# Ordinary units last in each phase, and more weight buffers, in a two-layer decoder trunk on one NeuronCore

## The chip, the cores and the metric

The kernel runs on one core of a Trainium2 chip. The metric is the device time of one execution in microseconds (us). The profile's engine names are PE (TensorE matmul), PEld (its weight loads), DVE (VectorE), ACT (ScalarE), POOL (GpSimd) and SP (SyncE, which issues most DMA here). PEclk is the TensorE clock that was granted, 1.00 being full speed.

## The reference

272 tokens (16 meta tokens and 256 input tokens) of width 2048 pass through two layers, each a token mixer (layer 0: RWKV-7, layer 1: gated linear attention) and a squared-ReLU MLP of hidden width 8192, all in float32:

```
def sq_relu_mlp(x, w1, w2):
    h = jax.nn.relu(x @ w1)
    return (h * h) @ w2

for i in range(DEPTH):                       # DEPTH = 2
    hn = rms_norm(h, norm_mix[i])
    h = h + (rwkv7_time_mix(hn, ...) if i % 2 == 0 else gla_time_mix(hn, ...))
    h = h + sq_relu_mlp(rms_norm(h, norm_mlp[i]), mlp_w1[i], mlp_w2[i])
return rms_norm(h, norm_f)[:, 16:]           # meta tokens dropped
```

Each MLP has two weight matrices of 2048 x 8192 (64 MiB each), so 256 MiB of MLP weights are read in one execution. The change touches the two MLPs and the final norm.

## The kernel before

**Stages.** The first mixer runs to about 592 us, the first MLP (`mlp`, L261) from 592 to 1350, the second mixer to about 1745, the second MLP (`mlp1`, L355) to about 2436, and the final norm and the store end it at 2450.8.

**Split weights.** Products are done to nearly float32 precision with rounded operands. A weight tile `raw` of 128 x 1024 floats (512 KB) is loaded by SP; ScalarE casts it to `hi` (the rounded value); VectorE makes `lo = raw - hi`. The data x is split in the same way, and TensorE adds up hi·xh, hi·xl and lo·xh (`mm3`, L162). So each tile passes DMA, ScalarE, VectorE and TensorE in this order. `wload` (L130) does the first three steps and takes the tiles from pool `wp`: three `raw` buffers and two sets of `hi` and `lo` in the first MLP.

**First MLP.** `up` and `down` go through 64 + 64 rows of output features; a row takes two weight tiles, each with 24 matmuls of 128 x 272: 256 tiles, 6144 matmuls. The order of the instructions on each engine is set by a scheduler that follows data dependences, buffers and priorities. Beside it runs `differences` (L314): for 48 units of the second MLP's w2 it has POOL's queue fetch three operands of 256 KB, VectorE subtract and add them (L335 to L337), and POOL's queue store the three results (`diff`) in memory. `tick` (L297) paces its 51 steps over 118 of the 128 rows; a unit's subtraction is written two steps after its fetch.

**Second MLP.** Here the order is written out. `stream` is a list of slots, each with a weight tile to load and a function that issues its matmuls; the loop at L569 does, for slot i, the functions due before it, the cast and the lo of slot i + 3, the functions due behind it, and the matmuls. There are two kinds of work. A *row* (`row`, L385) makes 128 hidden features: two slots, 16 pairs of matmuls 128 x 512 and 128 x 256 in PSUM bank `own[0]` (or 4), after which VectorE joins the halves (`cj`), squares are made (`F`), and operands for the second product are formed: `HS` with seven combinations for a fast unit, `HC` with four plain blocks for an ordinary one, each with a rounded and a low half. A *unit* (`unit`, L450) multiplies the hidden features of two rows by their part of w2. A *fast* unit does seven products of blocks (Strassen's scheme) instead of eight, with the operands that `differences` stored: banks 1, 2 (`pu`), 6, 7 (`pt`), 5 (`pm`), 3 (`pry`), 4 (`pj`), each product three matmuls. An *ordinary* unit does eight products in two slots, in banks 2, 3, 4 and 0. `FAST` lists the fast ones: 0, 1, 2, 4, 5, 6 of each eight; 3 and 7 are ordinary.

The work is in eight phases, b = 0 to 3 and g = 0, 1 (output columns 0 to 1023 and 1024 to 2047). In a phase, units 0 to 7 add up in their banks. With g = 0, row 10 + p of block b follows unit p for p < 6; with g = 1, row p of block b + 1 stands before unit p, and rows 8 and 9 behind unit 7; the last phase (b = 3, g = 1) has no rows. When the last fast unit is done, ScalarE copies bank 1 (`t1`) and VectorE combines banks 5, 6 and 7 into the result `htok` by eight adds of 128 x 512; after unit 7, it adds banks 2, 3 and 4 to `htok`. Bank 0, which the rows use too, is emptied after each ordinary unit.

**End.** In the last phase each emptied bank is squared and summed for the final norm (`final`, L443); then come, for token half 1 and then 0, sum and rsqrt (L584 to L589), scaling by VectorE and ScalarE (L594, L597) and eight stores (L599). The multiplication of columns 0 to 1023 by the norm's gain `nf` is done early, in `final`, as four operations of 128 x 512.

Of the kernel before, what the change touches and what calls it, by code (L numbers as in the profile page):

```python
# [18 lines left out]
P = 128  # L19
D = 2048  # L20
# [30 lines left out]
FAST = [0, 1, 2, 4, 5, 6]  # L51
# [5 lines left out]
class Kern:  # L57
    def __init__(self, ctx, tc, ap):
# [11 lines left out]
        self.wps = [self.wp]  # L70
# [59 lines left out]
    def wload(self, src, prio=2000):  # L130
        nc = self.nc
        with self.tc.high_priority(offset=prio) if prio else ExitStack():
            raw = self.t(self.wp, [P, 1024], "raw", self.raw_bufs)
# [3 lines left out]
            hi = self.t(pool, [P, 1024], "hi", self.hi_bufs, F32R)  # L137
            lo = self.t(pool, [P, 1024], "lo", self.hi_bufs, F32R)
# [122 lines left out]
    def mlp(self, layer, x, rstd, hres, off, done):  # L261
# [3 lines left out]
        with ExitStack() as es:  # L265
# [27 lines left out]

            steps = self.differences()
# [13 lines left out]
            down(NHB - 1, hid)  # L308

# [45 lines left out]
    def mlp1(self, x, rstd):  # L355
# [14 lines left out]
        hid, parts, before, behind = {}, {}, {}, {}  # L370
# [72 lines left out]
        def final(t, q, late=False):  # L443
# [3 lines left out]
            if not late:  # L447
                tt(h, h, nf[:, 512 * q : 512 * q + 512], ALU.mult)

        def unit(b, g, p):  # L450
# [36 lines left out]

            def pe(k):
                def run(w, slot):
                    H = hid[p]  # L490
                    order = ((2, 3, 4, 0), (2, 3, 0, 4) if end else (0, 2, 3, 4))[k]
                    for at in order:
                        h, ws = {2: (1, one), 0: (0, two), 3: (1, two), 4: (0, one)}[at]
                        product(at, (H[:, 0, 2 * k + h], H[:, 1, 2 * k + h]), w, ws, at == 0 and k == 0,
                                k == 1 and (at == 0 or last))
                    if k == 0:
                        return
                    outs = {2: (1, 0), 3: (1, 1), 0: (0, 1), 4: (0, 0)}
                    for n, at in enumerate(order):
                        if at == 0 or last:  # L500
                            def empty(at=at):
                                add(C[outs[at]], own[at], C[outs[at]])
                                if last and b == NHB - 1 and end:
                                    final(outs[at][0], 2 * g + outs[at][1], True)
# [1211 lines left out]
```

## Time and profile before

| what | us |
|---|---|
| median of 3 runs (lowest, highest) | 2450.61 (2448.34, 2451.45) |
| the profiled execution | 2452.58 |
| its span, first to last instruction | 2450.8 |
| first MLP, 592 to 1350 | 758 |
| one 173 us block of the second MLP: TensorE busy | 163.8 of 173.0 |
| last matmul starts | 2436.47 |

The mean granted TensorE clock is 0.99. A row of groups reads: line, engine, operation, output<-input, shapes, count | busy us, mean ns of one | idle time of the engine just before them <- what ended it. A row of waits: engine, what it was to do, <- what it waited for: us in all, times, longest. Names of tiles are given without their numbers. One line can be that of a helper: all adds of the second MLP carry L357, all casts of it L552.

### The profile page before, as it was taken

The numbers are of one execution on the slowest core, as the hardware profiler recorded it, in microseconds if no ns is written. First come the engines' busy times: TensorE is split into PE (matmuls) and PEld (weight loads), VectorE is DVE, ScalarE is ACT, GpSimd is POOL, SyncE is SP. The second block draws the span as 40 slices with busy tenths as digits, with TensorE's granted clock in tenths as the row PEclk, the third lists the DMA queues.
The fourth block names the chain that finished last, engine by engine and source line by source line (L and its number), as shares of the span: only waits on it lengthen the run. The fifth ranks groups of instructions, "written<-read, shape, count | busy, mean of one in ns | idle before, by whom it ended". The sixth has DMA issues, their size and how long they took to land.

```text
span 2450.8 us, 48648 instructions
## 1 busy us (share of the span) xinstructions
PE 2356.0 (96%) x19205; PEld 2196.8 (90%) x19205; DVE 1829.5 (75%) x3025; ACT 1332.0 (54%) x2075; POOL 206.5 (8%) x469
## 2 busy tenths in 40 slices
PE   9999999999999999999999999999999999998996
PEld 8888898889999999999999999999888888887885
DVE  8778977858666666666666777767678888888888
ACT  6487554666444344344334555655565565565565
POOL 0000000000223322323220000000000000000000
PEclk9999999999999999999999999999999999999998
DMA  6468754535888888888886655556576766676675
GB/s 207 153 214 297 229 168 137 150 103 183 267 291 286 303 286 294 286 296 297 283 280 199 196 175 179 164 166 202 201 233 226 243 226 228 219 250 223 223 249 181
DMA packets 194181, 550.95 MB, mean 225 GB/s; under 512 B 40160, under 2 KB 55776, under 8 KB 193824
## 3 DMA queue, kind: packets, MB, share of 16 engines
q1 hardware_dynamic: 170912, 472.33, 58.3%
q0 software_dynamic: 23040, 75.52, 9.6%
q8 instruction: 150, 2.46, 0.4%
q14 instruction: 79, 0.65, 0.1%
HBM read 493.89 MB, written 52.17 MB: 223 GB/s over the span
## 4 chain that ended last, share of the span: by engine, by line
PE 59%; DVE 18%; DMA 12%; ACT 5%; issue 4%; POOL 2%; SPq 0%; ACTq 0%; DVEq 0%; POOLq 0%
DMA raw<-mlp_w_d 11%; PE pj L396 9%; PE pj L167 9%; PE pj L165 9%; PE pj L166 9%; DVE lo L143 5%; PE pj L397 4%; ACT hi L142 3%; PE pj L198 2%; DVE lo L357 2%; DVE htok L357 1%; POOL x L329 1%; PE pj L199 1%; PE pu L457 1%; PE pu L458 1%
## 5 line engine op out<-in xcount | busy, mean ns | idle before, releaser
L142 ACT CAST hi<-raw 128x1024 fp32r<-128x1024 f32 (+1 forms) x562 | 526.1, 947 | 644.3 <-PE pj L166 364.3
L143 DVE TENSOR_TENSOR lo<-raw,hi 128x1024 fp32r<-128x1024 f32 (+1 forms) x562 | 613.5, 1101 | 336.5 <-ACT hi L142 330.4
L167 PE MATMUL pj<-x,lo 128*128 128x272 f32 (+1 forms) x2560 | 719.5, 281 | 16.3 <-DVE lo L143 15.5
L165 PE MATMUL pj<-x,hi 128*128 128x272 f32 (+1 forms) x2560 | 728.7, 285 | 3.2 <-ACT hi L142 1.6
L166 PE MATMUL pj<-x,hi 128*128 128x272 f32 (+1 forms) x2560 | 713.8, 279 | 0.5 <-DVE x L242 0.5
L167 PEld LDWEIGHTS pj<-x,lo 128*128 128x128 f32 x2560 | 484.8, 189 | 25.8 <-DVE lo L143 24.8
L165 PEld LDWEIGHTS pj<-x,hi 128*128 128x128 f32 x2560 | 484.8, 189 | 16.6 <-issue 6.5
L166 PEld LDWEIGHTS pj<-x,hi 128*128 128x128 f32 x2560 | 485.0, 189 | 3.2 <-issue 1.4
L357 DVE TENSOR_TENSOR lo<-raw,hi 128x1024 fp32r<-128x1024 f32 x352 | 396.5, 1148 | 80.5 <-ACT hi L552 78.5
L552 ACT CAST hi<-raw 128x1024 fp32r<-128x1024 f32 x352 | 338.6, 986 | 142.9 <-PE pj L396 77.8
L396 PE MATMUL pj<-x,hi 128*128 128x512 f32 x1024 | 347.6, 389 | 22.6 <-DVE htok L357 21.4
L167 PE MATMUL pj<-h,lo 128*128 128x272 f32 x1024 | 289.5, 283 | 10.8 <-DVE lo L143 10.0
L165 PE MATMUL pj<-h,hi 128*128 128x272 f32 x1024 | 286.3, 280 | 1.1 <-ACT hi L142 0.9
L166 PE MATMUL pj<-h,hi 128*128 128x272 f32 x1024 | 285.7, 279 | 0.0
L397 PE MATMUL pj<-x,lo 128*128 128x256 f32 x1024 | 282.2, 276 | 0.8 <-DVE lo L357 0.8
L396 PEld LDWEIGHTS pj<-x,hi 128*128 128x128 f32 x1024 | 196.8, 192 | 55.0 <-issue 16.3
L167 PEld LDWEIGHTS pj<-h,lo 128*128 128x128 f32 x1024 | 193.4, 189 | 17.5 <-DVE lo L143 17.2
L397 PEld LDWEIGHTS pj<-x,lo 128*128 128x128 f32 x1024 | 199.7, 195 | 2.2 <-DVE lo L357 1.1
L165 PEld LDWEIGHTS pj<-h,hi 128*128 128x128 f32 x1024 | 193.5, 189 | 2.3 <-ACT hi L142 2.3
L166 PEld LDWEIGHTS pj<-h,hi 128*128 128x128 f32 x1024 | 193.5, 189 | 0.0
L343 POOL DMA_DIRECT2D diff<-x x144 | 78.2, 543 | 129.5 <-DVE x L335 55.9
L198 PE MATMUL pj<-x,hi 128*128 128x512 f32 x256 | 84.1, 382 | 0.1
(361 smaller groups left out, 3450.8 us busy)
## 6 DMA issues: line engine op xcount, KB each, us to landing
raw<-mlp_w_d SPq DMA_DIRECT2D x384, 512.0 KB, 4.9
raw<-gla_in_d SPq DMA_DIRECT2D x98, 512.0 KB, 3.8
raw<-w_rkv_d SPq DMA_DIRECT2D x80, 512.0 KB, 4.4
raw<-w_d SPq DMA_DIRECT2D x80, 512.0 KB, 4.9
x<-w_d POOLq DMA_DIRECT2D x144, 256.0 KB, 5.8
diff<-x POOLq DMA_DIRECT2D x144, 256.0 KB, 6.3
raw<-diff SPq DMA_DIRECT2D x48, 512.0 KB, 5.5
raw<-gla_o_d SPq DMA_DIRECT2D x32, 512.0 KB, 4.3
```

Of the source, the lines that this page charges most:

```text
L142: nc.scalar.copy(hi[:, h], raw[:, h])
L143: nc.vector.tensor_tensor(out=lo[:, h], in0=raw[:, h], in1=hi[:, h].bitcast(F32), op=ALU.subtract)
L165: nc.tensor.matmul(out, hi[:, ws], xh, start=first, stop=False)
L166: nc.tensor.matmul(out, hi[:, ws], xl, start=False, stop=False)
L167: nc.tensor.matmul(out, lo[:, ws], xh, start=False, stop=last)
L198: nc.tensor.matmul(wide, hi[:, ws], xt, start=kt == 0, stop=False)
L199: nc.tensor.matmul(one, lo[:, ws], xt[:, 0], start=False, stop=kt == nk - 1)
L343: nc.gpsimd.dma_start(self.diff[b, g, i][:, k], x[:, body])
L357: tt = lambda o, a, b, op: nc.vector.tensor_tensor(out=o, in0=a, in1=b, op=op)
L396: nc.tensor.matmul(wide, hi[:, ws], xt, start=kt == 0, stop=False)
L397: nc.tensor.matmul(narrow, lo[:, ws], xt[:, 0], start=False, stop=kt == KT - 1)
L552: nc.scalar.copy(hi, raw)
```

## The change

1. *Units.* `FAST` becomes 0 to 5; the ordinary units are 6 and 7, last in each phase. They add to the sums that the fast units have left in banks 2, 3 and 4, and use bank 5, restarted once its fast result has been taken, instead of bank 0. All four are emptied once, after unit 7. Bank 0 belongs to the rows alone; row 9 of the next block uses bank 7 instead of 4. The adds behind the last fast unit are spread over slots +1 to +6.
2. *End.* In the last phase units 6 and 7 first do all products of token half 1 (banks 2 and 3), whose norm, scaling and stores then start (`gain`, `norm`); their products of half 0 (bank 5, then 4) come after. The gain of columns 0 to 1023 is multiplied here, 1024 wide, instead of in `final`.
3. *Buffers of the first MLP.* A new pool `wx` holds two more raw buffers and a third set of hi and lo.

```
-FAST = [0, 1, 2, 4, 5, 6]
+FAST = [0, 1, 2, 3, 4, 5]
...
     def wload(self, src, prio=2000):
...
-            raw = self.t(self.wp, [P, 1024], "raw", self.raw_bufs)
+            pool = self.raws[0]
+            self.raws = self.raws[1:] + [pool]
+            raw = self.t(pool, [P, 1024], "raw", self.raws.count(pool) if len(self.raws) > 1 else self.raw_bufs)
             nc.sync.dma_start(raw, src)
             pool = self.wps[0]
             self.wps = self.wps[1:] + [pool]
-            hi = self.t(pool, [P, 1024], "hi", self.hi_bufs, F32R)
-            lo = self.t(pool, [P, 1024], "lo", self.hi_bufs, F32R)
+            sets = self.wps.count(pool) if len(self.wps) == 3 else self.hi_bufs
+            hi = self.t(pool, [P, 1024], "hi", sets, F32R)
+            lo = self.t(pool, [P, 1024], "lo", sets, F32R)
...
+            wx = es.enter_context(tc.tile_pool(name="wx", bufs=1, side="right", reuse_waits="tile"))
+            self.raws, self.wps = [self.wp, wx, self.wp, wx, self.wp], [self.wp, self.wp, wx]
             steps = self.differences()
...
             down(NHB - 1, hid)
+            self.raws, self.wps = [self.wp], [self.wp]
...
                             if at == 5:
                                 later(slot + 2, lambda: (add(u4, own[5], u2), add(C[0, 1], own[5], C[0, 1])))
-                                later(slot + 3, lambda: (add(C[1, 0], C[1, 0], t1), add(C[0, 0], C[0, 0], u3)))
-                                later(slot + 4, lambda: (add(C[0, 1], C[0, 1], u3), add(C[1, 1], C[1, 1], u4)))
+                                later(slot + 3, lambda: add(C[1, 0], C[1, 0], t1))
+                                later(slot + 4, lambda: add(C[1, 1], C[1, 1], u4))
+                                later(slot + 5, lambda: add(C[0, 0], C[0, 0], u3))
+                                later(slot + (5 if end else 6), lambda: add(C[0, 1], C[0, 1], u3))
...
+            places = {2: (1, 0, 1, one), 3: (1, 1, 1, two), 5: (0, 1, 0, two), 4: (0, 0, 0, one)}
+
+            def ordinary(at, H, k, w, stop):
+                h, ws = places[at][2:]
+                product(at, (H[:, 0, 2 * k + h], H[:, 1, 2 * k + h]), w, ws, at == 5 and p == ORD[0] and k == 0, stop)
+
+            def empty(at):
+                t, f = places[at][:2]
+                add(C[t, f], own[at], C[t, f])
+                if end:
+                    final(t, 2 * g + f)
...
+                    if not end:
+                        for at in (2, 3, 4, 5):
+                            ordinary(at, H, k, w, last and k == 1)
+                        if last and k == 1:
+                            for n, at in enumerate((2, 3, 4, 5)):
+                                later(slot + 1 + n // 2, lambda at=at: empty(at))
...
+                    closing.append((H, k, w))
+                    for at in (2, 3):
+                        ordinary(at, H, k, w, last and k == 1)
+                    if last and k == 1:
+                        empty(2)
+                        empty(3)
+                        gain(1)
+                        norm(1)
+                        gain(0)
+                        for at in (5, 4):
+                            for n, (X, m, pair) in enumerate(closing):
+                                h, ws = places[at][2:]
+                                product(at, (X[:, 0, 2 * m + h], X[:, 1, 2 * m + h]), pair, ws, at == 5 and n == 0, n == 3)
+                            empty(at)
+                        norm(0)
...
+        def gain(t):
+            tt(htok[:, t, :1024], htok[:, t, :1024], nf[:, :1024], ALU.mult)
+
+        def norm(t):
...
+            for i, j in ((q, 0), (5 - q, 1)):
+                c, d = quarter[i], quarter[j]
+                nc.vector.scalar_tensor_tensor(out=h[:, c], in0=h[:, c], scalar=rt, in1=nf[:, c], op0=ALU.mult, op1=ALU.mult)
+                nc.scalar.mul(h[:, d], h[:, d], rt)
+                for y in (d, c):
+                    nc.sync.dma_start(out[:, y], h[:, y])
...
-                row(b + 1, 9, 4)
+                row(b + 1, 9, 7)
```

The order of the instructions shows three places. VectorE at the start of the first MLP, before (x are the split data operands, acc the sum of squares, pry a bank of the mixer's last product):

```order
L143 TENSOR_TENSOR lo_8293<-raw_8290,hi_8292 128x1024
L242 SCALAR_TENSOR_TENSOR x_7825<-hres_72,vecs_126,x_7825 128x272
L242 SCALAR_TENSOR_TENSOR x_7824<-hres_72,vecs_126,x_7824 128x272
L253 TENSOR_TENSOR acc_7826<-acc_7826,sq_8227 128x272
L605 TENSOR_TENSOR hres_72<-pry_8248,hres_72 128x272
L143 TENSOR_TENSOR lo_8323<-raw_8320,hi_8322 128x1024
L253 TENSOR_TENSOR acc_7826<-acc_7826,sq_8245 128x272
L242 SCALAR_TENSOR_TENSOR x_7817<-hres_72,vecs_126,x_7817 128x272
```

and in the change:

```order
L146 TENSOR_TENSOR lo_8296<-raw_8293,hi_8295 128x1024
L146 TENSOR_TENSOR lo_8364<-raw_8361,hi_8363 128x1024
L245 SCALAR_TENSOR_TENSOR x_7825<-hres_72,vecs_126,x_7825 128x272
L245 SCALAR_TENSOR_TENSOR x_7824<-hres_72,vecs_126,x_7824 128x272
L256 TENSOR_TENSOR acc_7826<-acc_7826,sq_8227 128x272
L632 TENSOR_TENSOR hres_72<-pry_8248,hres_72 128x272
L146 TENSOR_TENSOR lo_8326<-raw_8323,hi_8325 128x1024
L256 TENSOR_TENSOR acc_7826<-acc_7826,sq_8245 128x272
L245 SCALAR_TENSOR_TENSOR x_7817<-hres_72,vecs_126,x_7817 128x272
```

The third tile's lo (lo_8364) stands before the last three x operands; from here to the end of the stage every lo, and on ScalarE every cast, stands one tile further ahead. TensorE's order is the same in this stage.

VectorE at the end of a phase with g = 0, before (pt, pm, pu, pry, pj are the banks that it empties; HC is the low half of unit 7's operand; cj and z belong to row 15; lo are tiles ahead):

```order
L357 TENSOR_TENSOR HC_25176<-F_25078,HC_25176 128x512
L357 TENSOR_TENSOR hres_72<-pt_22401,hres_72 128x512
L357 TENSOR_TENSOR hres_72<-pt_22400,hres_72 128x512
L357 TENSOR_TENSOR lo_25209<-raw_25111,hi_25208 128x1024
L357 TENSOR_TENSOR lo_25222<-raw_25132,hi_25221 128x1024
L357 TENSOR_TENSOR hres_72<-pm_22402,hres_72 128x512
L357 TENSOR_TENSOR htok_22395<-pm_22402,htok_22395 128x512
L357 TENSOR_TENSOR lo_25233<-raw_25134,hi_25232 128x1024
L357 TENSOR_TENSOR htok_22395<-htok_22395,hres_72 128x512 x2
L357 TENSOR_TENSOR lo_25253<-raw_25156,hi_25252 128x1024
L357 TENSOR_TENSOR htok_22395<-htok_22395,hres_72 128x512 x2
L357 TENSOR_TENSOR htok_22395<-pj_22405,htok_22395 128x512
```

and in the change:

```order
L363 TENSOR_TENSOR htok_22399<-htok_22399,hres_72 128x512
L363 TENSOR_TENSOR cj_25188<-pj_22409,cj_25188 128x256
L423 SCALAR_TENSOR_TENSOR z_25189<-cj_25188,acc_22392 128x256
L363 TENSOR_TENSOR lo_25196<-raw_25109,hi_25195 128x1024
L363 TENSOR_TENSOR htok_22399<-htok_22399,hres_72 128x512
L363 TENSOR_TENSOR lo_25217<-raw_25124,hi_25216 128x1024
L363 TENSOR_TENSOR htok_22399<-htok_22399,hres_72 128x512
L363 TENSOR_TENSOR HC_25190<-F_25088,HC_25190 128x512
L363 TENSOR_TENSOR lo_25238<-raw_25136,hi_25237 128x1024
L363 TENSOR_TENSOR lo_25256<-raw_25147,hi_25255 128x1024
L363 TENSOR_TENSOR htok_22399<-pu_22403,htok_22399 128x512
L363 TENSOR_TENSOR htok_22399<-pry_22407,htok_22399 128x512
```

Before, HC came first and the fast units' adds, ending with the emptying of bank 0 (pj_22405), behind it; now those adds stand between the lo's, ahead of and around HC, and the ordinary banks follow it.

VectorE at the end of the program, before (rt is the rsqrt, hres holds the gain nf here):

```order
L357 TENSOR_TENSOR htok_22395<-pu_22399,htok_22395 128x512
L357 TENSOR_TENSOR htok_22395<-pry_22403,htok_22395 128x512
L357 TENSOR_TENSOR htok_22395<-pj_22405,htok_22395 128x512
L357 TENSOR_TENSOR htok_22395<-pj_22404,htok_22395 128x512
L357 TENSOR_TENSOR sum_3253_22397<-ssq_22396 128x1
L357 TENSOR_TENSOR sum_3253_22397<-sum_3253_22397,ssq_22396 128x1
L587 TENSOR_SCALAR sum_3253_22397<-sum_3253_22397 128x1
L594 SCALAR_TENSOR_TENSOR htok_22395<-htok_22395,rt_4519_28790,hres_72 128x512 x2
```

and in the change:

```order
L363 TENSOR_TENSOR htok_22399<-pu_22403,htok_22399 128x512
L363 TENSOR_TENSOR htok_22399<-pry_22407,htok_22399 128x512
L363 TENSOR_TENSOR htok_22399<-htok_22399,hres_72 128x1024
L363 TENSOR_TENSOR sum_3253_22401<-ssq_22400 128x1
L363 TENSOR_TENSOR sum_3253_22401<-sum_3253_22401,ssq_22400 128x1
L548 TENSOR_SCALAR sum_3253_22401<-sum_3253_22401 128x1
L555 SCALAR_TENSOR_TENSOR htok_22399<-htok_22399,rt_4516_28752,hres_72 128x512 x2
L363 TENSOR_TENSOR htok_22399<-htok_22399,hres_72 128x1024
L363 TENSOR_TENSOR htok_22399<-pm_22406,htok_22399 128x512
L363 TENSOR_TENSOR htok_22399<-pj_22408,htok_22399 128x512
```

The scaling of token half 1 (L555) now stands ahead of the emptying of the last two banks; sums and scaling of half 0 follow, as before.

More of the change, by code (lines that the diff above doesn't have):

```diff
@@ L69, in __init__ @@
         self.split_parts = 1
-        self.wps = [self.wp]
+        self.wps, self.raws = [self.wp], [self.wp]
     def nm(self, s):
@@ L369, in mlp1 @@
                                                                 self.pj, self.pj))}
-        hid, parts, before, behind = {}, {}, {}, {}
+        hid, parts, before, behind, closing = {}, {}, {}, {}, []
+        ORD = [p for p in range(KT // 2) if p not in FAST]
         one, two, both = slice(0, 512), slice(512, 1024), slice(0, 1024)
@@ L490, in run @@
                     H = hid[p]
[L491 to L496, printed above, removed]
-                        return
-                    outs = {2: (1, 0), 3: (1, 1), 0: (0, 1), 4: (0, 0)}
@@ L499, in run @@
[L499 to L504, printed above, removed]
-                            later(slot + 1 + n // 2, empty)
-                    if last and b == NHB - 1 and g == 0:
-                        for n in range(4):
-                            later(slot + 4 + n, lambda n=n: final(n // 2, n % 2))
+                    if not end:
[4 more added lines that the diff above has]
+                                later(slot + 1 + n // 2, lambda at=at: empty(at))
+                            if b == NHB - 1:
+                                for n in range(4):
+                                    later(slot + 4 + n, lambda n=n: final(n // 2, n % 2))
+                        return
```

32 lines of the change are left out of this document (10 added, 22 removed).

## The prediction

> **What bounds the kernel now.** The page comes first: TensorE is busy 96% of the span, so a gain has to come out of the 4% in which it stands, out of stretches in which it is "busy" at a lower pace, or out of the tail.
>
> ```profile
> PE 2356.0 (96%) x19205; PEld 2196.8 (90%) x19205; DVE 1829.5 (75%) x3025; ACT 1332.0 (54%) x2075; POOL 206.5 (8%) x469
> ```
>
> The windows come next, cut at the stages (first MLP; one 173 us block of the second; last phase with the tail) and around single waits. The columns are busy time of the five engines, PEclk, DMA share, GB/s.
>
> ```profile
> core 0: us, PE busy (x) PEld busy (x) DVE busy (x) ACT busy (x) POOL busy (x), PEclk, DMA share, GB/s
> 592.00:1350.00 758.00, 733.30 (x6140) 717.59 (x6139) 486.66 (x625) 329.29 (x420) 194.46 (x432) 1.00 0.82 278
> 900.00:950.00 50.00, 49.75 (x419) 48.77 (x418) 33.14 (x45) 24.09 (x34) 13.41 (x30) 1.00 0.87 306
> 1300.00:1350.00 50.00, 50.00 (x434) 50.00 (x433) 31.84 (x46) 25.67 (x37) 0.00 (x0) 1.00 0.58 187
> 1800.00:1850.00 50.00, 49.55 (x269) 44.25 (x268) 42.98 (x59) 32.22 (x42) 0.00 (x0) 1.00 0.78 268
> 1868.00:2041.00 173.00, 163.81 (x861) 144.99 (x860) 145.24 (x191) 101.30 (x130) 0.00 (x0) 0.97 0.71 231
> 2389.00:2451.00 62.00, 41.14 (x175) 34.00 (x173) 50.02 (x68) 31.38 (x50) 0.00 (x0) 0.87 0.54 180
> 2043.00:2053.00 10.00, 5.83 (x21) 5.15 (x22) 7.55 (x11) 0.87 (x2) 0.00 (x0) 0.66 0.55 192
> 2089.00:2095.00 6.00, 4.54 (x27) 3.82 (x26) 3.79 (x6) 2.09 (x2) 0.00 (x0) 1.00 0.37 115
> 2126.00:2134.00 8.00, 5.82 (x20) 4.48 (x19) 7.25 (x11) 3.14 (x5) 0.00 (x0) 0.79 0.65 219
> ```
>
> In the first MLP the stretch without differences() (1300 to 1350) shows the unhindered pace: 50 / 434 = 0.1152 us a matmul. At that pace its 6140 matmuls take 707.4 us; they take 758.0. So **50.6 us** are lost there, more than the 24.7 us in which PE is idle, because a late weight load stretches matmuls too. Who is late: the waits of 592 to 1350, and the groups of the same window.
>
> ```profile
> PE pj L167 <- DVE lo L143: 20.3, 41, 0.8
> PEld pj L167 <- DVE lo L143: 34.4, 63, 1.0
> L142 ACT CAST hi<-raw 128x1024 fp32r<-128x1024 f32 x257 | 268.8, 1046 | 425.4 <-PE pj L166 209.8 <-DMA raw<-mlp_w_d 192.2 <-issue 10.2
> L143 DVE TENSOR_TENSOR lo<-raw,hi 128x1024 fp32r<-128x1024 f32 x256 | 313.4, 1224 | 235.8 <-ACT hi L142 234.2
> L335 DVE TENSOR_TENSOR x<-x,x 128x513 f32<-128x513 f32 x48 | 33.3, 693 | 7.3 <-POOL x L334 5.9
> ```
>
> TensorE waits for lo, VectorE waits for ScalarE's hi, and ScalarE waits in about equal parts for TensorE to give a hi/lo set back and for the raw tile to land. The second MLP's waits name another cause:
>
> ```profile
> PE pj L396 <- DVE htok L357: 21.4, 10, 5.1
> PE pj L457 <- DVE cj L357: 6.5, 3, 2.2
> PE pu L457 <- DVE htok L357: 5.5, 1, 5.5
> ```
>
> These are PSUM banks that VectorE has not emptied. Three instances, in the timeline (start, length, instruction, idle before it):
>
> ```profile
> 2045.13 1.29 DVE L357 TENSOR_TENSOR htok<-htok,hres 128x512 f32<-128x512 f32 x2
> 2046.33 0.69 DVE L357 TENSOR_TENSOR htok<-pj,htok 128x512 f32<-128x512 f32 x1
> 2047.17 0.77 PE L396 MATMUL pj<-x,hi 128*128 128x512 f32 x1 [5.06 <-DVE htok L357]
> 2129.93 0.48 PE L457 MATMUL pj<-hi,HC 128*128 128x512 f32 x1 [2.18 <-DVE cj L357]
> 2395.23 0.80 PE L457 MATMUL pu<-hi,HS 128*128 128x512 f32 x1 [5.52 <-DVE htok L357]
> ```
>
> At 2046.33 the add that frees the row's bank 0 stands at the end of the burst of adds that closes a phase.
>
> **Term A, first MLP: two more raws, a third set.** A tile lasts TensorE 24 x 0.1152 = 2.76 us. A raw buffer is held from its issue until lo has read it. The landing rows of 600 to 1290:
>
> ```profile
> DMA to landing us min/median/max: 3.5/5.7/8.6
> DMA packets 56328, 197.39 MB, mean 286 GB/s; under 512 B 8296, under 2 KB 8296, under 8 KB 56264
> x<-w_d POOLq DMA_DIRECT2D x144, 256.0 KB, 5.8
> ```
>
> Median: 5.7 + 1.05 (cast) + 1.22 (lo) = 8.0 us, against 3 x 2.76 = 8.3 for three buffers; at the 8.6 maximum it is 10.9, so every slow landing reaches TensorE. Five buffers allow 13.8. A set is held 1.05 + 1.22 + 2.76 = 5.0 us against 5.5 for two sets; three allow 8.3. The same casts and subtractions run, one tile earlier, so nothing is added. I leave 3 us for landings that bunch up.
>
> What this part adds stands at its start. VectorE now makes the third tile's lo ahead of the last three x operands; the second tile's stays, as before, ahead of the last, x_7817:
>
> ```profile
> 592.62 1.23 DVE L143 TENSOR_TENSOR lo<-raw,hi 128x1024 fp32r<-128x1024 f32 x1
> 594.12 0.50 DVE L242 SCALAR_TENSOR_TENSOR x<-hres,vecs,x 128x272 fp32r<-128x272 f32 x1
> 594.67 0.38 PE L166 MATMUL pj<-x,hi 128*128 128x272 f32 x1 [0.50 <-DVE x L242]
> ```
>
> In the before, one lo (592.62) already precedes x_7817 (594.12), and TensorE waits 0.50 us. One cast of 1.05 and one lo of 1.23 more, with an x pair behind them that was early, make about 2.6 us of further wait, 3.1 in all, so -2.6; bounds 0 (the third raw is there early and all slides forward) and -4.3 (with 1.7 us at half clock). A = 50.6 - 3 - 2.6 - 1.05 (one cast at the end, where the added pool gives its place back to the next stage) = **44**; bounds 20 (next rival) and 49.
>
> The clock after a wait: the 1.46 us wait inside 2089 to 2095 leaves PEclk at 1.00; the 2.18 us one is followed by 0.79 over 8 us, the 5.06 us one by 0.66 over 10 us. [...]
>
> **Term B, second MLP: bank 0 left to the rows.** The 13 waits on bank 0 (21.4 + 6.5) make 27.9 us. The half-clock stretches: 10 x (1 - 0.66) = 3.4 and 8 x (1 - 0.79) = 1.7, 5.1 us a block, three times 15.3. Cross-check by pace, from the first matmuls of a unit, the row behind it and the next unit:
>
> ```profile
> 2012.60 0.38 PE L457 MATMUL pu<-hi,HS 128*128 128x512 f32 x1
> 2017.13 0.38 PE L396 MATMUL pj<-x,hi 128*128 128x512 f32 x1
> 2022.37 0.38 PE L457 MATMUL pu<-hi,HS 128*128 128x512 f32 x1
> ```
>
> A fast unit is 4.53 us, a row 5.24, an ordinary unit 24 / 21 of a fast one, 5.18: 12 x 4.53 + 4 x 5.18 + 16 x 5.24 = 158.9 for a block that takes 173.0 (1868 to 2041); the 14.1 too much are the waits (27.9 / 3 = 9.3) and the clock (5.1) to within 0.3. B = **43.2** if nothing takes their place; 36 if a third of the clock drops stays with other waits.
>
> **Term C, what takes their place.** The six closing adds (0.60 us each from start to start, as at 2045.13 and 2046.33) now lie between VectorE's lo's instead of ahead of a row. But in the half-phases g=0 unit 7's low half (HC) now stands behind four of them. After row 15's last matmul: join and z to about 1.6 us; the set for the next cast is free only when unit 6's first half has run (2.6 + 0.3), cast to 4.0, lo to 5.2, add to 5.8, HC to 6.6 us. TensorE wants it after unit 6 and one matmul, 5.18 + 0.4. So about 1.1 us late, in four phases: **-4.4**; bounds 0 (casts come sooner) and -15 (2 us each, the clock drop of 1.7 behind each). Queued behind HC are two lo's of the next unit, one unit ahead of need. Bank 5's restart, row 9's bank 7 and the bank 0 of the row are emptied a row (5.24 us) before use: nothing. One add less a phase (0.69 us x 8) runs beside TensorE: nothing.
>
> **Term D, last phase and tail.** Now 2388.90 to 2450.8, 61.9 us:
>
> ```profile
> 2388.90 0.38 PE L457 MATMUL pu<-hi,HS 128*128 128x512 f32 x1
> 2422.11 3.62 ACT L552 CAST hi<-raw 128x1024 fp32r<-128x1024 f32 x4 [2.41 <-DMA raw<-diff]
> 2432.68 1.22 DVE L357 TENSOR_TENSOR lo<-raw,hi 128x1024 fp32r<-128x1024 f32 x1
> 2436.47 0.38 PE L459 MATMUL pj<-hi,HC 128*128 128x512 f32 x1
> 2441.96 4.46 SPq L599 DMA_DIRECT2D out_d<-htok  x8
> ```
>
> Gone: the 5.52 us wait and some 2.6 us of half clock behind it, the mean of the two drops above (3.4 and 1.7). Units without rows between them run out of raws already now (2422.11: 2.41 us for a landing), and six follow each other instead of three: I give back a part of one more such wait, 1.5. From the end of the last lo (2433.90) to the end it is 16.9 us now. In the changed kernel: six adds 3.6, the 1024-wide multiply 1.1, sums and rsqrt for token half 1 about 1.0, two scalings 1.4, the second multiply 1.1, two adds 1.2, square and rsqrt 1.6, scalings 1.4, then issue to end as now (last issue 2445.83 of 2450.8, 5.0, and 0.6 to reach it): 18.0. The first half's store is hidden, the second half's chain is longer by its multiply. D = 5.5 + 2.6 - 1.5 + 0.1 = 6.7; bounds 2 and 10.
>
> **Sum.** 44 + 43.2 - 4.4 + 6.7 = 89.5. The profiled execution took 2452.58 (span 2450.8), 2.0 above the median of 2450.61: 2452.6 - 89.5 = 2363.1, and against the median 2361. I say **2362 us**.
>
> **Rivals.**
> R1, the memory sets the first MLP's pace. For: the DMA engines are 87% busy at 306 GB/s in the best quoted stretch; A asks for 197.4 MB in 690 - 40 us, 304 GB/s, over the whole stage. Against: the 306 were reached with buffers that stood waiting. If 295 is all, 197.4 MB need 669 us of the 690: gain 21, 23 less than A: **2385**. Chance 0.14.
> R2, slower: the deeper weight queue holds up POOL's fetches. differences() (L314, L295) takes 51 steps over 118 rows of 48 x 0.1152 = 5.53 us, 12.8 us a step, and subtracts two steps after the fetch: 25.6 us, against a landing of 5.8 us now; L335 idles 5.9 us for it over 48 units. From 25.6 us on, each unit's subtraction stalls VectorE with the lo's behind it; at 28 us that is 48 x 2.4 = 115 us: 2361 + 115 = **2476**. Against: it needs landings five times as long. [...] Chance 0.03.
> R3, VectorE becomes the bound of the long fast runs of the second MLP. In 1800 to 1850 it is busy 86%, 8.4 us of the 9.77 of a fast unit and a row, and what is left must hold its waits for casts; but TensorE is busy 49.55 of 50 there, through three such pairs in a row, which speaks against. If in the 42 fast units that have a row beside them the lo's slip by one add (0.69 us), 29 us go: **2390**. Chance 0.07.
> R4, the buffers are there but not used: the order has casts and lo's only one tile further on, so of the two causes in ScalarE's idle time only one is mended. A is then half of 50.6, 25, and the time **2380**. Chance 0.10.
>
> **How the numbers follow.** The forecast has 0.66, R1 0.14, R4 0.10, R3 0.07, R2 0.03. The forecast's own range, with A between 38 and 49 and C and D at their bounds, is 2350 to 2377. R1, R4 and R3 lie below 2392; the range of 8 in 10 is **2349 to 2392**. A measurement of this kernel tells about 0.2%, 5 us, from no change. Faster 0.95, same 0.02, slower 0.03 (R2).
>
> **What would show it.** Right: the first MLP about 714 us long, the waits on lo there down to a few us; no row of waits on htok at the rows' matmuls; PEclk 1.00 through a block and a block of about 160 us; a wait on HC of about 1 us at unit 7 in four phases; one wait of 2 to 3 us on an x operand at the first MLP's start; the last phase 55 us. Wrong: a first MLP above 730 us with ScalarE still waiting for raw landings (R1) or for TensorE (R4), L335 waiting for POOL (R2), PE waiting for lo in the second MLP (R3), or a tail whose chain on VectorE is longer than 18 us.

## The result, and the profile after

The changed kernel takes **2366.7 us** (median of 4 runs, 2364.6 to 2367.97), the kernel before 2451.03 in the same comparison: a ratio of **0.9655** with a 95% interval of 0.9638 to 0.9671. The forecast was 2362, with a range of 2349 to 2392. Medians here and below are over the undisturbed runs that the ratios use.

The profiled execution took 2366.46, its span 2364.7, 86.1 less than before. The page's first lines and the windows of the changed kernel (columns as before):

```profile
span 2364.7 us, 48731 instructions
...
PE 2321.2 (98%) x19205; PEld 2182.1 (92%) x19205; DVE 1826.4 (77%) x3015; ACT 1331.5 (56%) x2075; POOL 189.7 (8%) x469
```

```profile
592.00:1306.00 714.00, 713.53 (x6155) 712.99 (x6153) 493.60 (x628) 331.30 (x423) 177.62 (x432) 1.00 0.85 295
900.00:950.00 50.00, 50.00 (x434) 50.00 (x434) 36.44 (x48) 25.58 (x36) 14.83 (x36) 1.00 0.90 311
1713.00:1874.50 161.50, 159.92 (x894) 143.91 (x893) 136.53 (x183) 104.19 (x139) 0.00 (x0) 1.00 0.72 241
2308.00:2365.00 57.00, 41.75 (x175) 33.19 (x173) 44.37 (x58) 31.17 (x49) 0.00 (x0) 0.89 0.56 186
```

The busy times of VectorE and ScalarE are what they were (1829.5 and 1332.0 us before); TensorE does the same 19205 matmuls with 34.8 us less busy time and stands 51.3 us less. In the first MLP, 50 us now hold 434 matmuls in the stretch with differences() too, the pace that only 1300 to 1350 had before. A block of the second MLP is 161.5 us instead of 173.0, with a clock of 1.00. The norm matmul of each layer gives two exact marks for the first MLP, first of before, then of the changed kernel:

```profile
595.24 0.68 PE L257 MATMUL pm<-acc,cst 128*128 128x272 f32 x2
...
1355.06 0.67 PE L257 MATMUL pm<-acc,cst 128*128 128x272 f32 x2
```

```profile
595.02 0.68 PE L260 MATMUL pm<-acc,cst 128*128 128x272 f32 x2
...
1306.33 0.73 PE L260 MATMUL pm<-acc,cst 128*128 128x272 f32 x2 [0.34 <-DVE acc L256]
```

759.8 became 711.3: **48.5 us** came from here. The groups of that stage show the cast's idle time with its causes:

```profile
L145 ACT CAST hi<-raw 128x1024 fp32r<-128x1024 f32 x257 | 268.9, 1046 | 380.3 <-PE pj L169 376.3 <-PE pj L170 1.1 <-issue 1.0
L341 DVE TENSOR_TENSOR x<-x,x 128x513 f32<-128x513 f32 x48 | 33.4, 696 | 12.3 <-POOL x L340 10.7
```

Of the 192.2 us of waiting for landings 0.9 are left; ScalarE waits for TensorE in 377.4 of its 380.3 us, and TensorE is busy in 713.53 of 714.00. L341 (L335 before) waits 10.7 us for POOL, 5.9 before.

The waits of TensorE from 1680 on, and the place where unit 7 starts (VectorE has no idle time in these rows):

```profile
PE pu L464 <- DVE HC L363: 5.9, 4, 1.5
PE pm L463 <- DVE lo L363: 2.0, 4, 0.8
PE pj L404 <- DVE lo L363: 1.5, 4, 0.8
PE pm L462 <- ACT hi L598: 1.3, 1, 1.3
PE pj L403 <- ACT hi L598: 1.2, 1, 1.2
```

```profile
1810.46 0.38 PE L462 MATMUL pu<-hi,HC 128*128 128x512 f32 x1
...
1812.48 0.69 DVE L363 TENSOR_TENSOR htok<-htok,hres 128x512 f32<-128x512 f32 x1
1813.08 0.42 DVE L363 TENSOR_TENSOR cj<-pj,cj 128x256 f32<-128x256 f32 x1
...
1817.35 0.68 DVE L363 TENSOR_TENSOR HC<-F,HC 128x512 fp32r<-128x512 f32 x1
1818.09 0.48 PE L464 MATMUL pu<-hi,HC 128*128 128x512 f32 x1 [1.48 <-DVE HC L363]
...
1822.94 0.38 PE L403 MATMUL pj<-x,hi 128*128 128x512 f32 x1
```

The waits on htok, 26.9 us before, are gone but for one of 0.3; the wait on HC stands where the forecast put it. Units 6 and 7 take 12.48 us (1810.46 to 1822.94) instead of 10.37. Row 15 ends at 1810.46, but its join starts only at 1813.08, behind adds and lo's.

### The profile page after: what moved, and what is told of

Same layout as the page of the kernel before. It is cut to its first block, busy times and chain, and to the rows that moved or that the text cites. A ratio compares the mean times of both kernels' runs of the same rounds, so it can differ in the third digit from the quotient of the medians.

```text
span 2364.7 us, 48731 instructions
## 1 busy us (share of the span) xinstructions
PE 2321.2 (98%) x19205; PEld 2182.1 (92%) x19205; DVE 1826.4 (77%) x3015; ACT 1331.5 (56%) x2075; POOL 189.7 (8%) x469
## 4 chain that ended last, share of the span: by engine, by line
PE 80%; DVE 13%; ACT 3%; issue 2%; DMA 2%; SPq 0%; DVEq 0%; ACTq 0%; POOL 0%; POOLq 0%
PE pj L168 16%; PE pj L170 16%; PE pj L169 15%; PE pj L403 8%; PE pj L404 4%; PE pj L201 2%; DVE lo L146 2%; DVE lo L363 2%; PE pj L202 1%; DVE upd L632 1%; PE pu L464 1%; DVE sysA L632 1%; ACT hi L145 1%; PE pu L462 1%; PE pu L463 1%
## 5 line engine op out<-in xcount | busy, mean ns | idle before, releaser
L168 PEld LDWEIGHTS pj<-x,hi 128*128 128x128 f32 x2560 | 484.8, 189 | 14.8 <-issue 6.5
L170 PEld LDWEIGHTS pj<-x,lo 128*128 128x128 f32 x2560 | 484.9, 189 | 6.9 <-DVE lo L146 6.6
L169 PEld LDWEIGHTS pj<-x,hi 128*128 128x128 f32 x2560 | 485.0, 189 | 2.5 <-issue 1.4
L403 PE MATMUL pj<-x,hi 128*128 128x512 f32 x976 | 325.7, 384 | 1.2 <-ACT hi L598 1.2
L404 PE MATMUL pj<-x,lo 128*128 128x256 f32 x976 | 267.2, 274 | 1.5 <-DVE lo L363 1.5
L403 PEld LDWEIGHTS pj<-x,hi 128*128 128x128 f32 x976 | 185.2, 190 | 27.2 <-ACT hi L598 1.5
L404 PEld LDWEIGHTS pj<-x,lo 128*128 128x128 f32 x976 | 187.9, 193 | 4.1 <-DVE lo L363 2.7
L201 PE MATMUL pj<-x,hi 128*128 128x512 f32 x256 | 84.1, 382 | 0.1
```

The source lines that it names most:

```text
L168: nc.tensor.matmul(out, hi[:, ws], xh, start=first, stop=False)
L169: nc.tensor.matmul(out, hi[:, ws], xl, start=False, stop=False)
L170: nc.tensor.matmul(out, lo[:, ws], xh, start=False, stop=last)
L201: nc.tensor.matmul(wide, hi[:, ws], xt, start=kt == 0, stop=False)
L403: nc.tensor.matmul(wide, hi[:, ws], xt, start=kt == 0, stop=False)
L404: nc.tensor.matmul(narrow, lo[:, ws], xt[:, 0], start=False, stop=kt == KT - 1)
```

## The experiments

The kernel before was run again beside each group of kernels; its medians were 2449.3 and 2448.5 us there, 2451.0 beside the changed kernel. A difference of some 3 us between two kernels is therefore also read from the traces.

**The first MLP without the pool, and with one half of it.** Three kernels tell what the buffers bring, and which of them. Without the pool:

```
-            wx = es.enter_context(tc.tile_pool(name="wx", bufs=1, side="right", reuse_waits="tile"))
-            self.raws, self.wps = [self.wp, wx, self.wp, wx, self.wp], [self.wp, self.wp, wx]
```

> The changed kernel without the added pool: three raw buffers and two hi/lo sets in the first MLP, all else as changed. The stage between the two norm matmuls lasts 759.8 us in the kernel before and 711.3 in the changed one. If the buffers are what shortened it: 711.3 + 48.5, so about 2415 us in all, the second MLP unchanged. If the stage became shorter through anything else: below 2390.

Measured: 2414.0 us, ratio to before 0.9852 (0.9837 to 0.9867); the stage, between the same marks:

```profile
594.50 0.68 PE L260 MATMUL pm<-acc,cst 128*128 128x272 f32 x2
...
1352.03 0.62 PE L260 MATMUL pm<-acc,cst 128*128 128x272 f32 x2
```

757.5 us. The buffers bring 46 to 47 us, and nothing else shortened the stage by more than 2.3. With five raws and two sets (`self.wps = [self.wp]`):

> The changed kernel with the five raw buffers and only two hi/lo sets. Theory 1, landings: the loop of a raw buffer (5.7 + 1.05 + 1.22 = 8.0 us) was at the limit of three buffers (8.3) and the set's loop (5.0 of 5.5) was not; then this one keeps nearly all of the gain, 2367 to 2373 us. Theory 2, both limits count about half, as ScalarE's idle time in the kernel before divides (209.8 for TensorE, 192.2 for landings): about 2390. Theory 3, the set alone: about 2410.

Measured: 2371.0 us, ratio 0.9682 (0.9666 to 0.9699).

```profile
597.28 0.63 PE L260 MATMUL pm<-acc,cst 128*128 128x272 f32 x2
...
1311.33 0.62 PE L260 MATMUL pm<-acc,cst 128*128 128x272 f32 x2
```

714.1 us: theory 1, the raws alone bring 43 of the 46 between 757.5 and 711.3. With three raws and three sets (`self.raws = [self.wp]`):

> The changed kernel with three raw buffers and three hi/lo sets. Theory 1, landings: nearly nothing of the gain is left, 2405 to 2416 us. Theory 2, both: about 2390. Theory 3, the set alone: 2367 to 2375.

Measured: 2391.2 us, ratio 0.9747 (0.9724 to 0.977). That is theory 2's number, beside theory 1's for the raws: the two gains, some 43 and 23, add up to more than the whole. So neither theory was right about the set. What the set does to the stage itself:

> The changed kernel with three raws and three sets, to see its first MLP. Five raws alone left the stage at 714.1 us, the kernel without both at 757.5. If depth counts wherever it stands between the loads and TensorE: a stage of 730 to 740 us, with ScalarE waiting for landings for 50 to 120 us (192 before) and less for TensorE. If the set's loop was a limit of its own: landings wait as before, near 190 us, and TensorE's waits for lo fall all the same.

Measured: 2387.5 us (two runs), ratio 0.975 (0.973 to 0.9771). The groups of the stage in this kernel, and its end (it starts at 597.52):

```profile
L145 ACT CAST hi<-raw 128x1024 fp32r<-128x1024 f32 x261 | 272.4, 1046 | 356.6 <-DMA raw<-mlp_w_d 266.8 <-PE pj L169 59.8 <-PE pj L170 17.1
...
1329.41 0.73 PE L260 MATMUL pm<-acc,cst 128*128 128x272 f32 x2 [0.38 <-DVE acc L256]
```

The stage is 731.9 us, in the range of the depth theory, but ScalarE's wait for landings did not fall as that theory had it; it rose from 192 to 267 us, while TensorE's waits for lo fell from 20.3 to 9.0 us. The third set lets ScalarE start as soon as a tile has landed, instead of waiting for TensorE to return a set (this wait fell from 209.8 to 76.9 us); so it stands at the landings more of the time (the rise), and TensorE can have one more converted tile in reserve when a landing is late (its waits fell). The second half of this is argued from the waits, not measured by itself. A split of a waiting time by its last cause (209.8 and 192.2 us) therefore did not say what each cause is worth.

**The pool alone, in the kernel before.** The same lines of `wload` and `mlp`, nothing else:

> The kernel before with the added pool alone (five raws, three sets in the first MLP), nothing else changed. If the parts are independent, as the sum takes them: the first MLP 711 us, all else as before, 2451 - 48.5 = 2402 us, and its gain and that of the kernel without the pool add up to the whole. If the second MLP or the mixer between lost by it: above 2405.

Measured: 2404.3 us, ratio 0.982 (0.9806 to 0.9834). Its marks stand at 596.55 and 1307.83, 711.3 us. The pool alone brings 44 us against the runs beside it (2448.5), the rest alone 35 (2414.0 against 2449.3); their sum is 79 to 80 of the 84 in all. The spans of the profiled executions give 48.2 and 40.9, 89 of 86. The parts are independent to within some 5 us, which is about what two such differences can tell.

**Bank 0 shared again, the adds spread.**

```
-            places = {2: (1, 0, 1, one), 3: (1, 1, 1, two), 5: (0, 1, 0, two), 4: (0, 0, 0, one)}
+            X0 = 5 if end else 0
+            places = {2: (1, 0, 1, one), 3: (1, 1, 1, two), X0: (0, 1, 0, two), 4: (0, 0, 0, one)}
...
+                        for at in ((2, 3, 4, 0), (0, 2, 3, 4))[k]:
+                            ordinary(at, H, k, w, k == 1 and (last or at == 0))
+                        if k == 1:
+                            for n, at in enumerate((0, 2, 3, 4) if last else (0,)):
+                                later(slot + 1 + n // 2, lambda at=at: empty(at))
```

> The changed kernel, but units 6 and 7 use bank 0 in place of bank 5 again (not in the last phase), and it is emptied after each of them as in the kernel before; the closing adds stay spread. If the sharing of the bank is the cause of the waits: each ordinary unit is followed by a user of bank 0 that waits 1.5 to 2.2 us, some 12 to 14 waits, with a drop of the clock behind those of 2 us: 2390 to 2405 us. If the burst of adds ahead of the emptying was the cause, and the shared bank itself costs little: 2367 to 2375.

Measured: 2383.4 us, ratio 0.9727 (0.9711 to 0.9743), 16.7 more than the changed kernel: between the two theories. Its waits from 1702 to 2317, and one block of 167 us (161.5 in the changed kernel):

```profile
PE pj L403 <- DVE htok L363: 9.4, 9, 1.5
PE pj L462 <- DVE cj L363: 8.5, 7, 1.5
PE pu L464 <- DVE HC L363: 1.9, 3, 0.6
...
1869.00:2036.00 167.00, 159.98 (x856) 141.54 (x856) 144.07 (x189) 100.67 (x129) 0.00 (x0) 1.00 0.71 239
```

There are sixteen waits on bank 0, where 12 to 14 were expected, but the longest is 1.5 us, and the clock stays at 1.00. So the waits of 5 us and the clock's drops (15.3 us) need more than the shared bank. Two other things differ in the kernel before: the burst of adds, and the place of the ordinary units, which puts the burst right before unit 7's bank is needed. These runs do not separate them. In the rows of the kernel before, the burst's double adds stand directly ahead of both kinds of wait, at 2045.13 for the one of 5.06 us and here for the one of 2.18 us (at 2129.93):

```profile
2128.25 1.29 DVE L357 TENSOR_TENSOR htok<-htok,hres 128x512 f32<-128x512 f32 x2
2129.45 0.42 DVE L357 TENSOR_TENSOR cj<-pj,cj 128x256 f32<-128x256 f32 x1
```

**The adds in a burst, bank 0 private.**

```
-                                later(slot + 3, lambda: add(C[1, 0], C[1, 0], t1))
-                                later(slot + 4, lambda: add(C[1, 1], C[1, 1], u4))
-                                later(slot + 5, lambda: add(C[0, 0], C[0, 0], u3))
-                                later(slot + (5 if end else 6), lambda: add(C[0, 1], C[0, 1], u3))
+                                later(slot + 3, lambda: (add(C[1, 0], C[1, 0], t1), add(C[0, 0], C[0, 0], u3)))
+                                later(slot + 4, lambda: (add(C[0, 1], C[0, 1], u3), add(C[1, 1], C[1, 1], u4)))
```

> The changed kernel with the four last closing adds at their old places, two and two, instead of one by one; rows keep bank 0 to themselves. Together with the run in which bank 0 is shared and the adds are spread, this fills a table of two by two (both old: the kernel before, 43 us of waits and clock; shared bank and spread adds: 16.7 us). If the burst hurts only because the emptying of bank 0 stands behind it, it costs nothing with a bank of its own: 2365 to 2369 us. If the burst by itself delays the lo's and HC: 5 to 15 us more, 2372 to 2382.

Measured: 2370.6 us, ratio 0.9681 (0.9665 to 0.9698): 3.9 more than the changed kernel, just above the first theory's range. The waits on HC from 1702 to 2317:

```profile
PE pu L462 <- ACT HC L443: 5.2, 4, 1.3
PE pu L464 <- DVE HC L363: 2.6, 4, 0.6
```

Three of its four pairs of units 6 and 7 take 14.53 or 14.54 us and one 12.85, where the changed kernel's take 12.48 and 12.83. Longer waits account for some 0.4 us of a pair; the rest is a lower clock behind the waits of three of them (0.72 over 6 us, 1.7 us each; last section), which neither theory had.

The table of two by two, all with the pool: private and spread 2366.7, private and burst 2370.6, shared and spread 2383.4, shared and burst 2404.3 (the kernel before with the pool, which also has the old place of the ordinary units and the old end, so that the 20.9 us between the last two are not the burst's alone). The private bank is the larger part; the spread pays mainly where something waits behind the adds.

**HC earlier.** HC's cast and low half one slot earlier, for ordinary units only:

```
+                early = p not in FAST
...
-                later(slot + 2, lambda: nc.scalar.copy(H[:, 0], src), True)
-                later(slot + 3, lambda: tt(H[:, 1], src, H[:, 0].bitcast(F32), ALU.subtract))
+                later(slot + 2 - early, lambda: nc.scalar.copy(H[:, 0], src), True)
+                later(slot + 3 - early, lambda: tt(H[:, 1], src, H[:, 0].bitcast(F32), ALU.subtract))
```

> The changed kernel, but HC, the operand of the ordinary units, is cast and its low half made one slot earlier, ahead of one closing add and one lo. In the changed kernel the pair of units 6 and 7 takes 12.48 us in three phases and 12.83 in one, 10.37 at the bare pace. If HC's place in VectorE's order is the cause: pairs of 10.4 to 10.8 us, 7 to 8 us less in all, 2359 to 2361. If VectorE is simply behind there (row 15's join already starts 2.6 us after the row's end), the wait only moves on to the lo that now comes later: 2364 to 2367.

Measured: 2358.9 us, ratio 0.9635 (0.9622 to 0.9647), 7.8 less. The waits of TensorE from 1713 to 2310:

```profile
PE pj L404 <- DVE lo L363: 0.8, 3, 0.4
PE pu L465 <- DVE HC L363: 0.5, 1, 0.5
PE pm L463 <- DVE htok L363: 0.3, 1, 0.3
```

The pair takes 10.74 us in three phases and 11.09 in one, 7.0 us less in all. It was HC's place in the queue: the lo's that now stand behind it cost only 0.2 us in each of four phases, at a row that takes 5.44 us instead of 5.24. What is left of the 7.8 these runs do not assign; one drop of the clock, which the changed kernel's trace has at the second MLP's start and this one does not (last section), is as large, 1.7 us.

**Six raw buffers in the second MLP.** `free` 6 instead of 5, three buffers in each pool:

> The changed kernel with six raw buffers instead of five in the second MLP. In its last phase the six fast units take 34.9 us, 27.2 at their pace of 4.53, and ScalarE waits 9.3 us for raw tiles to land. If the loop of five buffers is too short there (landing 5.5 to 6.1 + cast 1.05 + lo 1.22 + the wait for the second tile of the pair, about 8.5 us, against 5 x 1.51 = 7.6; six give 9.1): 5 to 7 us less, 2360 to 2362. If the memory's rate or VectorE sets that pace: 2365 to 2367. Elsewhere nothing changes by either.

Measured: 2363.5 us, ratio 0.9652 (0.9639 to 0.9664), 3.2 less, half of what was expected. The waits of the last phase, of the changed kernel and then with six buffers:

```profile
ACT hi L598 <- DMA raw<-diff: 7.8, 5, 2.9
DVE lo L363 <- ACT hi L598: 5.1, 6, 2.1
```

```profile
ACT hi L598 <- DVE raw L363: 4.8, 5, 1.2
PEld pu L463 <- DVE lo L363: 2.7, 3, 1.2
...
ACT hi L598 <- DMA raw<-w_d: 1.2, 2, 0.8
```

The cause was right: the wait for landings nearly goes (from 9.3 to 1.8 us), and the six fast units take 29.0 us. But the 34.9 us from which 5 to 7 us were expected are the longest of the traces with five buffers; 1.7 us of them are a drop of the clock:

```profile
2338.00:2344.00 6.00, 5.10 (x15) 4.00 (x16) 5.79 (x7) 5.06 (x7) 0.00 (x0) 0.72 0.51 173
```

With five buffers as well, the six units take 32.3 us in the kernel without the pool (first matmuls 2354.15 to 2386.41), 32.7 in the one with five raws and two sets (2318.19 to 2350.85) and 32.4 in the one with HC early (2300.95 to 2333.32). Units 6 and 7 take 12.1 us with six buffers, since TensorE waits there for VectorE's lo's, and 10.4 in the changed kernel; but those three kernels show 12.0 to 12.1 too, so this wait is not the sixth buffer's doing. All eight units together take 41.1 us with six buffers, 45.3 in the changed kernel and 44.3 to 44.8 in the other three: 3.2 to 4.2 us less, which agrees with the medians.

**The old order of products at the end.**

```
-                    for at in (2, 3):
+                    for at in (2, 3, 5, 4):
                         ordinary(at, H, k, w, last and k == 1)
...
-                            for n, (X, m, pair) in enumerate(closing):
-                                h, ws = places[at][2:]
-                                product(at, (X[:, 0, 2 * m + h], X[:, 1, 2 * m + h]), pair, ws, at == 5 and n == 0, n == 3)
```

> The changed kernel, but units 6 and 7 of the last phase issue their products in the order of the other phases (banks 2, 3, 5, 4 for each tile); VectorE's order is as in the changed kernel. TensorE then reaches the last products of banks 2 and 3 only after 24 - 6 products that now come later. If TensorE's order matters, the first scaling starts 1.5 to 2.5 us later and so does the end: 2368 to 2370. If VectorE's chain alone sets the end: 2366 to 2367.

Measured: 2370.0 us, ratio 0.9684 (0.967 to 0.9697), 3.3 more, as the first theory had it: TensorE's order of products matters. The last products of banks 2 and 3 then stand behind 18 other matmuls (24 - 6), 3.9 us at the pace of 4.53 / 21 a matmul; that most of this reaches the end is argued from the two numbers, as no trace here shows it.

**Both improvements, and the gain's multiplication earlier.** First HC early and six raws:

> HC early and six raw buffers together. If both causes are as supposed, they are at different places and add up: 2353 to 2356 us. If only one holds: 2359 to 2362.

Measured: 2355.3 us, ratio **0.9620** (0.9608 to 0.9632): the two add up (7.8 + 3.2 = 11.0, measured 11.4), and this version is faster than both kernels. Then the gain as well:

```
+                                for n in range(2):
+                                    later(slot + 9 + n, lambda n=n: gain(n))
...
-                        gain(1)
...
-                        gain(0)
```

> HC early, six raws in the second MLP, and the multiplication of columns 0 to 1023 by the norm's gain done in the first units of the last phase, as far ahead as in the kernel before, instead of in the closing chain. The second multiplication of 1.2 us lies on the chain ahead of the last two adds, the first beside ScalarE's squares. If the last phase ends by VectorE's chain: 1.1 to 1.8 us less than HC and six raws alone (2356.7), 2355. If the end hangs on TensorE's last products (bank 4): no change.

Measured: 2356.1 us, ratio 0.9621 (0.9607 to 0.9634): no difference that these runs can tell. The two profiles show where it went. From the end of the last lo to the end of the span it is 15.4 us (2338.55 to 2354.0) instead of 17.6 (2337.31 to 2354.9), as expected and a little more. But the six fast units, among which the two multiplications now stand on VectorE, take 30.6 us instead of 28.9 (first matmuls 2302.15 to 2332.70, and 2302.52 to 2331.38). So work moved within the phase was paid at the other place. That VectorE's list sets the pace there with six buffers is a reading of this, not tested by itself.

## Why the prediction was right, and where it was off

**By terms** (us of the span; marks as above; the second MLP's rows begin at 1739.88 before and 1691.01 now, its last phase at 2388.90 and 2307.99):

| term | forecast | measured | from |
|---|---|---|---|
| A, first MLP | 44 | 48.5 | 759.8 - 711.3 |
| B, bank 0 | 43.2 | 44.0 | what is left: rows to last phase 649.0 - 617.0 = 32.0, and 12.0 that C and the clock took |
| C, HC late | -4.4 | -10.3 | pairs 3 x 2.11 + 2.46, three rows of 5.74 for 5.24 |
| clock at the second MLP's start | 0 | -1.7 | last section |
| D, last phase and tail | 6.7 | 5.2 | 61.9 - 56.7 |
| sum | 89.5 | 86.1 | with 0.4 in the mixers |

That the sum is off by only 3.4 us is in part luck: A brought 4.5 us more than forecast, C cost 5.9 more. Three of the forecast's own figures do not come out of its terms. A third of the clock drops is 5.1 us, so B's lower value is 38, not 36. With A at 38 and C and D at their lower bounds the terms give 68.2, and 2384, not 2377, ends its own range. D's is below.

**A** was right in its mechanism, and the raw loop against three buffers was the right sum: the run with five raws and two sets shows that the raws carry nearly all. Two sizes in it were off. Of the 2.6 us of new wait at the stage's start about half came, and it stands before the mark from which the 48.5 us are counted. The rows show it, the first of the kernel before, the others of the changed kernel (the first two are the same matmul of both):

```profile
593.43 0.28 PE L167 MATMUL pj<-x,lo 128*128 128x272 f32 x1
...
591.97 0.28 PE L170 MATMUL pj<-x,lo 128*128 128x272 f32 x1
588.38 2.36 DVE L146 TENSOR_TENSOR lo<-raw,hi 128x1024 fp32r<-128x1024 f32 x2 [0.43 <-ACT hi L145]
591.33 1.04 ACT L145 CAST hi<-raw 128x1024 fp32r<-128x1024 f32 x1 [0.88 <-DMA raw<-mlp_w_d]
593.17 0.38 PE L168 MATMUL pj<-x,hi 128*128 128x272 f32 x1 [0.46 <-ACT x L244]
```

Up to there the changed kernel is 1.46 us ahead, from the first mixer; at the norm matmul (595.02 for 595.24) only 0.22, so some 1.2 us were lost between. The third tile's lo ran at once behind the first tile's (588.38, two in a row), when the x operands behind it were not yet due. The second tile's cast then waited 0.88 us for its landing, and TensorE waits for the x that ScalarE makes behind that cast, not for x_7817. Counted from the mixer's end, A is therefore some 47 us. The kernel before with the pool alone loses 1.1 us at the same place (593.64 and then 596.55). The hand-over at the end cost nothing visible. What the forecast had no ground for is the split of the casts' idle time in R4, "of the two causes only one is mended": in the runs with one half of the pool the raws mend nearly all, and the set alone about half, of what both mend together.

**B** held: bank 0's waits and the clock drops behind them are gone to the last (PEclk is 1.00 from 1713 to 2308), and the block came down to the pace of its parts plus the new waits (158.9 + 2.1 + 0.5 = 161.5). Of its 43 us, the runs give the shared bank by itself 16.7. The 5 us waits and all the drops needed the burst ahead of the emptying or the old place of the ordinary units, which the runs do not part; the rows of the kernel before speak for the burst.

**C** is the step that was mis-sized: 1.1 us a phase forecast, 2.1 to 2.5 measured, and half a microsecond at row 6 that the forecast did not have. The chain "after row 15's last matmul: join and z to about 1.6 us" took VectorE to be free at the row's end. It was behind by then, with the adds of banks 6, 7 and 5, two closing adds and four lo's ahead of the join since 1804.74; the join came at 1813.08, 2.6 us after the row, and not at about 1811.2 (the forecast's 1.6 us less the join and z). The cast, which the forecast made the brake, was not: VectorE was busy without a gap. Moving HC up takes 7.0 us off the four pairs by the order alone, which settles it.

**D**: the wait of 5.5 us and its clock drop (PEclk 0.50 from 2394 to 2400 before) went. The stretch of six fast units lost 7.7 us (34.9 for 27.2) where the forecast gave back 1.5 beyond what was there before. 1.7 of it is a new drop of the clock (2338 to 2344), and six buffers show most of the rest to be the raw loop, as the forecast said, only larger. The tail from the last lo's end (2347.07) is 17.6 us, 18.0 forecast. By the forecast's own figures the tail grows by 1.1 (18.0 for 16.9), while its sum adds 0.1; with -1.1 it would have had D = 5.5, beside 5.2 measured.

**The rivals.** R1: 311 GB/s in 900 to 950 with TensorE at its full pace, so the memory was no bound at this rate. R2: POOL's fetches land in 5.8 us as before and L341 waits 10.7 us over 48 units; the fetches were not held up. R3: the waits for lo in the second MLP are 3.7 us in all (2.0 + 1.5 + 0.2). R4: ScalarE waits 0.9 us for landings of `mlp_w` in the first MLP, 192.2 before.

## What to carry to other kernels

Here a buffer loop that fitted the median landing (8.0 of 8.3 us) still left ScalarE waiting 192.2 us for landings, the slowest of which took 8.6; depth between the load and the bound engine bought the loss back, 43 of 46 us in raw buffers alone and 26 in converted sets alone, and the split of an engine's waiting time by cause did not say how much each was worth. Before costing a wait behind moved work, ask how far behind the engine already is at that moment, from its rows with no gap; then put the one operand that the bound engine needs next ahead of the adds that nobody awaits.

## What was not expected of the hardware

The same two waits had two outcomes. At the start of the second MLP TensorE waits 1.17 and 0.78 us in both of the following profiles; in that of the changed kernel the clock drops behind them, in that of the kernel with HC earlier it does not:

```profile
1697.00:1701.00 4.00, 4.00 (x14) 3.48 (x15) 3.46 (x3) 1.83 (x2) 0.00 (x0) 0.58 0.71 194
```

```profile
1697.50:1701.50 4.00, 3.91 (x25) 3.65 (x26) 3.94 (x6) 3.13 (x5) 0.00 (x0) 1.00 0.67 223
```

In the kernel with the burst, one program repeats a pair of waits (1.31 and 0.64 us) in each block; in the first the clock stays, in the later ones it drops:

```profile
1816.84 0.48 PE L462 MATMUL pu<-hi,HC 128*128 128x512 f32 x1 [1.31 <-ACT HC L443]
1979.15 0.48 PE L462 MATMUL pu<-hi,HC 128*128 128x512 f32 x1 [1.31 <-ACT HC L443]
...
1817.00:1823.00 6.00, 5.36 (x24) 4.39 (x25) 3.54 (x5) 1.78 (x2) 0.00 (x0) 1.00 0.77 264
1979.50:1985.50 6.00, 5.36 (x17) 4.12 (x16) 2.08 (x3) 1.40 (x2) 0.00 (x0) 0.72 0.74 258
2143.00:2149.00 6.00, 5.36 (x17) 4.07 (x17) 2.20 (x3) 1.40 (x2) 0.00 (x0) 0.72 0.74 262
```

The fourth phase drops as well (0.72 in 2306 to 2312). Nor is a single wait of 2.18 us, which dropped the clock three times in the kernel before, always followed by a drop. The kernel before with the pool alone has it three times, at 1908.63, 2081.70 and 2255.45; the clock stays at the first and drops at the other two:

```profile
1904.00:1912.00 8.00, 5.82 (x28) 4.58 (x26) 7.42 (x11) 3.31 (x5) 0.00 (x0) 1.00 0.63 208
2078.00:2086.00 8.00, 5.82 (x20) 4.48 (x19) 7.39 (x11) 2.92 (x4) 0.00 (x0) 0.79 0.65 211
```

So some 2 us of idle time, in one wait (2.18 us) or in two close together (1.17 and 0.78, 1.31 and 0.64), were followed by a drop in some instances and not in others; what decides between them no trace here shows. The waits of up to 1.5 us in the kernel with bank 0 shared show none (its block above has a clock of 1.00). The forecast's reading of one trace, that a wait of 2.18 us is followed by a drop, does not hold for every instance. The drop of 0.28 over 6 us is 1.7 us. The changed kernel's, read in steps of 1 us, is as large: from 1697 to 1702 the clock reads 0.83, 0.50, 0.50, 0.50 and 0.97.
